# Gather, running sum and product: converting gathers into 64 slots instead of float32 gathers with casts on ScalarE

## The chip, the cores and the metric

The kernel runs on one core of one Trainium2 chip. The time is the device time of one execution in microseconds (us); of several executions the median is given. Beside it there is one execution taken by the hardware profiler, and all durations of single instructions come from that one.

The core has these engines, each with its own instruction stream: TensorE (PE in the profile, with its weight loads as PEld) multiplies matrices, VectorE (DVE) and ScalarE (ACT) work element by element, GpSimd (POOL) here issues the gathers, and SyncE (SP) issues the stores. 16 DMA engines move data between the main memory (HBM) and the on-chip memory (SBUF). Engines wait for each other through semaphores.

## The reference

```python
def reference(x, indices, w):        # x: 16 x 4096 x 512 float32, indices: 16 x 2048, w: 512 x 512
    B, S, D = x.shape
    b_idx = np.arange(B)[:, None]
    gathered = x[b_idx, indices, :].copy()
    cs = np.cumsum(gathered, axis=1)
    return np.matmul(cs, w).astype(np.float32)
```

For each of 16 batches 2048 rows are picked from 4096 by a sorted list of indices, summed up from the first row on, and each running sum is multiplied by `w`. 67.1 MB are read by the gathers and 67.1 MB are written.

## The kernel before, in words

The 16 x 2048 rows are 256 tiles (`T`) of 128 rows; a batch is 16 tiles (`NT`, also `U`, the length of a loop pass). Two tiles make a pair (`R = 2`, group `g`). In a pair the rows are not in tile order: the mask `ut` and the layout of `cst` deal them out so that each partition of the output holds two neighbouring rows, 4 KB in a row in HBM. In the first and the last pair (`PLAIN`, line 146) rows stay in order (mask `uq`), so that a tile can be finished without its partner.

A tile goes through these steps:

- `gather` (lines 127 to 143, GpSimd): one indirect DMA reads 128 rows of 2 KB into a float32 slot of `g32`. There are 16 slots (`NG`). From tile 16 on, the gather waits until the tile that last used its slot's pair has been cast (semaphore `s_c`, line 130).
- `cast` (lines 148 to 154, ScalarE): float32 to float16 into `g16` (8 pairs). The tables `casts` and `cast_by` (lines 114 to 125) say which casts come ahead of which drain; a cast runs up to 10 tiles (`FAR`) ahead of the drain.
- `sums` (lines 156 to 171, TensorE): four 128 x 128 products of the tile's columns with the mask give the running sums inside the tile, transposed, in PSUM buffer `pa` (four).
- `carry` (lines 173 to 198, VectorE): adds the last sum of the tile before and writes float16 into `cst`.
- `project` (lines 200 to 215, TensorE): four products with `w16`, 512 columns each, into PSUM buffer `pb` (four).
- `drain` (lines 217 to 220, ScalarE): copies `pb` to the output buffer `ob` (8 pairs).
- `store` (lines 222 to 236, SP): one DMA of 512 KB per pair, in the first and last pair one of 256 KB per tile. ScalarE waits for the store of eight pairs before (`s_o`, line 385) when it begins to refill a pair of `ob`.

The order on TensorE is written out ahead (lines 338 to 346): `lead` is how many tiles `sums` runs ahead of `project`, up to 4, less at both ends. On ScalarE the order is: wait for the slot of `ob` (at every second tile), the casts due, the drain. GpSimd's program is the 256 gathers in tile order. The middle of each program is a loop: 16 tiles a pass on TensorE, VectorE and ScalarE; the first and last tiles are written out.

Of the kernel before, what the change touches and what calls it, by code (L numbers as in the profile page):

```python
# [7 lines left out]
P = 128  # L8
FP32 = mybir.dt.float32
FP16 = mybir.dt.float16  # L10
# [23 lines left out]
def kernel(  # L34
# [7 lines left out]
    nc = tc.nc  # L42

    B, S, D = x.shape
    N = indices.shape[1]
    R = 2
# [15 lines left out]
    NO = 8  # L62
    U = NT
    assert U % NG == 0 and U % (R * NO) == 0 and U % NA == 0 and U % (R * NC) == 0 and U % NB == 0
    assert D == 512 and N % (R * P) == 0 and T % P == 0

    x_flat = x.rearrange("b s d -> (b s) d")
# [1 line left out]
    const = ctx.enter_context(tc.tile_pool(name="const", bufs=1))  # L69
# [31 lines left out]
    s_el = [sem(f"s_el{j}") for j in range(R)]  # L101
    s_ol = [sem(f"s_ol{j}") for j in range(R)]
    s_g = [sem(f"s_g{i}") for i in range(NG)]
# [10 lines left out]
    casts = []  # L114
    cast_by = []
    for u in range(T):
        far = min(FAR, 2 + u // 4, 2 + (T - 1 - u) // 4)
        casts.append([])
        while len(cast_by) <= min(u + far, T - 1):
            n = R if far > 4 and len(cast_by) % R == 0 else 1  # L120
            casts[u].append((len(cast_by), n))
            cast_by += [cast_by[-1] + 1 if cast_by else 1] * n

    for u in range(3 * U, T - 2 * U):
        assert casts[u] == [(t + U, n) for t, n in casts[u - U]]

    def gather(t):
        g, r = divmod(t, R)
        if t >= NG:
            pool.need(s_c, cast_by[R * (g + 1) - NG - 1])  # L130
        if t < FIRST:
            pool.need(s_first[g], 16)
            ap = idx_first[:, t, 0:1]
        else:
            pool.need(s_prep, t // P + 1)
            ap = idxg[:, t // P, t % P : t % P + 1]
        nc.gpsimd.indirect_dma_start(  # L137
            out=g32[g % (NG // R)][:, r, :],
            out_offset=None,
            in_=x_flat,  # L140
            in_offset=bass.IndirectOffsetOnAxis(ap=ap, axis=0),
            element_offset=(t // NT) * S * D,
        ).then_inc(s_g[t % NG], 16)


    PLAIN = (0, G - 1)

    def cast(t, n, first=None):
        g, r = divmod(t, R)
        for u in range(t, t + n):  # L150
            act.need(s_g[u % NG], 16 * (u // NG + 1), first)
        nc.scalar.copy(  # L152
            out=g16[g % NH][:, r : r + n], in_=g32[g % (NG // R)][:, r : r + n]
        ).then_inc(s_c, 1)

    def sums(t, u, first=None):
        g, r = divmod(t, R)
        tiles = None if first is None else R * first
        pe.need(s_c, cast_by[t] if first is None else cast_by[2 * U + t] - 2 * U // R, first)
        pe.need(s_d, t - NA + 1, tiles)  # L160
        for c in range(DC):
            if c == 1 and u is not None:
                pe.need(s_e, u - NB + 1, tiles)
            mm = nc.tensor.matmul(  # L164
                out=pa[t % NA][:, c],
                lhsT=g16[g % NH][:, r, c * P : (c + 1) * P],
                rhs=uq[:] if first is None and g in PLAIN else ut[:],
                start=(c == 0),
                stop=(c == DC - 1),
            )  # L170
        mm.then_inc(s_a, 1)
# [28 lines left out]
    def project(u, t, first=None):  # L200
        g, j = divmod(u, R)
        tiles = None if first is None else R * first
        pe.need(s_e, u - NB + 1, tiles)
        pe.need(s_d, u + 1 if first is None and g in PLAIN else R * (g + 1), tiles)
        for c in range(DC):
            if c == 2 and t is not None:
                pe.need(s_d, t - NA + 1, tiles)
            mm = nc.tensor.matmul(  # L208
                out=pb[u % NB][:],
                lhsT=cst[g % NC][:, c, j, :],  # L210
                rhs=w16[:, c, :],
                start=(c == 0),
                stop=(c == DC - 1),
            )
        mm.then_inc(s_b, 1)

    def drain(u, first=None):
        g, j = divmod(u, R)
        act.need(s_b, u + 1, first)
        nc.scalar.copy(out=ob[g % NO][:, j], in_=pb[u % NB][:]).then_inc(s_e, 1)  # L220

    def store(g):
        b, h = divmod(g, GB)
        rows = out[b, h * R * P : (h + 1) * R * P, :]
        if g in PLAIN:
            for j in range(R):
                sp.need(s_e, R * g + j + 1)
                done = s_ol[j] if g else (s_o[0], s_of)[j]
                nc.sync.dma_start(
                    out=rows[j * P : (j + 1) * P, :], in_=ob[g % NO][:, j]  # L230
                ).then_inc(done, 16)
# [24 lines left out]
    for g in range(G):  # L256
        store(g)
    for g in range(G - NO, G - 1):
        sp.need(s_o[g % NO], 16 * (g // NO + 1))
    for j in range(R):  # L260
        sp.need(s_ol[j], 16)


    nc.gpsimd.memset(ident[:], 1.0).then_inc(s_ut, 1)
# [3 lines left out]
        out=ident[:],  # L268
        in_=ident[:],
# [7 lines left out]
        out=ut[:],  # L277
# [72 lines left out]
    step = 2 * U  # L350
    for i in range(head + step, tail):
        assert order[i] == (order[i - step][0], order[i - step][1] + U)

    def run(i, first=None):
        is_sums, t = order[i]
        after = next((v for k, v in order[i + 1 :] if k != is_sums), None)
        if first is not None:
            t -= 2 * U
            after -= 2 * U
        if is_sums:  # L360
            sums(t, after, first)
        else:
            pe.need(s_wc, DC)
            project(t, after, first)

    for i in range(head):
        run(i)
    with nc.tensor.Fori(2 * U // R, (T - 2 * U) // R, U // R) as first:
        pe.new_pass()
        for i in range(head, head + step):  # L370
            run(i, first)
# [7 lines left out]
        act.need(s_w[c], 16)  # L379
        nc.scalar.copy(out=w16[:, c, :], in_=w32[:, c, :]).then_inc(s_wc, 1)  # L380
    def step(u, first=None):
        if u % R == 0:
            if first is None and u == R * NO:
                act.need(s_of, 16)
# [44 lines left out]
```

## Time and profile before

| | |
|---|---|
| Median of three runs | 454.9 us (454.53 to 455.43) |
| The profiled execution | 449.29 us, of which the span from first to last instruction is 447.5 us |
| Mean granted TensorE clock | 0.881 of full speed |
| TensorE, matmuls | busy 340.6 us, 76% of the span |
| ScalarE | busy 259.6 us: 256 drains of 0.598 us mean, 139 casts, 138.0 us in all |
| GpSimd | busy 243.9 us: 256 gathers, 0.946 us each |
| VectorE | busy 178.5 us |
| DMA | 135.69 MB, mean 303 GB/s |

How to read it: busy time is the time in which an engine executes; a wait is the time in which it stood before an instruction, with the one that released it. "remote", or "another core or an unknown queue", means that the profile has no record of the releaser; on one core it is a queue whose end was not recorded, or a wait that left no trace. A DMA share is the busy part of the 16 engines together. The page's rows of slices cut the span into 40 equal parts of 11.2 us, each digit in tenths. A busy engine need not be the bound: what counts is which wait ends last.

### The profile page before, as it was taken

The page shows a single profiled execution, that of the slowest core. Times are in us where ns is not written, and L with a number is a line of the kernel's source. Part 1 is how long each engine was busy: PE and PEld are TensorE (multiplying, and loading weights), DVE is VectorE, ACT ScalarE, POOL GpSimd, SP SyncE. Part 2 cuts the span into 40 slices and gives each one's busy share as a digit, 9 for nine tenths or more (in the row PEclk, how much of TensorE's full clock was granted, in tenths as well). Part 3 has the DMA queues.
Part 4 walks back from the last instruction along what each step waited for, and adds up shares of the span by engine and source line. Part 5 has one row for each costly group of instructions (what it writes and reads, how often), then busy time and mean ns, then how long its engine had stood idle before and what let it go on. Part 6 is the DMA issues. An engine that isn't in the chain of part 4 may idle for free.

```text
span 447.5 us, 6498 instructions
## 1 busy us (share of the span) xinstructions
PE 340.6 (76%) x2066; PEld 170.5 (38%) x2066; DVE 178.5 (40%) x263; ACT 259.6 (58%) x399; POOL 243.9 (54%) x266
## 2 busy tenths in 40 slices
PE   6354687578858887868788877987588888787995
PEld 2111244244424443424344434444244444344552
DVE  3103344224423454443345433444334444343652
ACT  3212467356636676655567655676456666555984
POOL 6771466575556555655656555655556655555300
PEclk9756789796999698988989889889889889799999
DMA  7874589897899888999989899988898988899974
GB/s 231 255 237 146 187 273 338 312 323 264 311 339 322 298 320 313 343 330 325 326 307 346 313 349 325 327 307 302 334 321 316 333 315 299 313 353 332 336 320 187
DMA packets 40619, 135.69 MB, mean 303 GB/s; under 512 B 6816, under 2 KB 7072, under 8 KB 40608
## 3 DMA queue, kind: packets, MB, share of 16 engines
q0 software_dynamic: 20480, 67.13, 47.3%
q1 hardware_dynamic: 19568, 67.91, 37.7%
q10 hardware_dynamic: 560, 0.53, 0.4%
q8 instruction: 5, 0.08, 0.1%
q14 instruction: 6, 0.05, 0.0%
HBM read 68.42 MB, written 67.11 MB: 303 GB/s over the span
## 4 chain that ended last, share of the span: by engine, by line
PE 70%; issue 12%; another core or an unknown queue 7%; ACT 6%; DVE 3%; DMA 1%; POOL 0%; ACTq 0%; DVEq 0%; SPq 0%
PE pb L208 54%; PE pa L164 16%; ACT g L152 3%; ACT ob L220 3%; DVE cst L196 3%; DMA g<-in_x_dram,idx_first 1%; DMA idx_first<-in_indices_dram 0%; DVE cst L183 0%; POOL g L137 0%; ACTq L26 0%; DVEq L26 0%; ACTq L393 0%; SPq L424 0%; SPq L90 0%
## 5 line engine op out<-in xcount | busy, mean ns | idle before, releaser
L137 POOL DMA_INDIRECT g<-in_x_dram,idxg x252 | 238.4, 946 | 173.1 <-ACT g L152 106.4
L208 PE MATMUL pb<-w,cst 128*128 128x512 f16 x1024 | 297.7, 417 | 44.0 <-issue 21.8
L196 DVE TENSOR_TENSOR cst<-pa,cst 128x512 f16<-128x512 f32 x240 | 166.0, 692 | 241.3 <-PE pa L164 152.4
L220 ACT COPY ob<-pb 128x512 f32<-128x512 f32 x256 | 144.9, 598 | 178.2 <-PE pb L208 118.8
L164 PE MATMUL pa<-ut,g 128*128 128x128 f16 x1008 | 113.1, 233 | 55.0 <-issue 21.3
L208 PEld LDWEIGHTS pb<-w,cst 128*128 128x128 f16 x1024 | 95.2, 106 | 126.2 <-issue 48.0
L152 ACT CAST g<-g 128x1024 f16<-128x1024 f32 (+1 forms) x139 | 138.0, 994 | 0.8 <-DMA g<-in_x_dram,idx_first 0.8
L164 PEld LDWEIGHTS pa<-ut,g 128*128 128x128 f16 x1008 | 81.5, 105 | 137.5 <-issue 45.5
L183 DVE CAST cst<-pa 128x512 f16<-128x512 f32 x16 | 11.0, 688 | 15.6 <-PE pa L164 14.0
L304 PE MATMUL pb<-zeros 128*128 128x512 f16 x16 | 5.7, 521 | 1.5 <-DVE zeros L308 1.5
L137 POOL DMA_INDIRECT g<-in_x_dram,idx_first x4 | 4.0, 994 | 1.6 <-issue 0.9
L304 PEld LDWEIGHTS pb<-zeros 128*128 128x128 f16 x16 | 1.9, 127 | 4.0 <-issue 1.9
L164 PE MATMUL pa<-uq,g 128*128 128x128 f16 x16 | 1.6, 220 | 1.7 <-ACT g L152 0.9
L377 ACT ACT_TABLE_LOAD x1 | 1.3, 1283 | 2.5 <-issue 2.5
L380 ACT CAST w<-w 128x512 f16<-128x512 f32 x2 | 1.1, 614 | 2.7 <-DMA w<-in_w_dram 2.7
L311 DVE CAST idxf<-idx 128x128 f32<-128x128 uint32 x2 | 0.5, 264 | 4.2 <-DMA idx<-in_indices_dram 4.2
L164 PEld LDWEIGHTS pa<-uq,g 128*128 128x128 f16 x16 | 1.0, 97 | 3.0 <-ACT g L152 1.5
L325 DVE CAST w<-w 128x512 f16<-128x512 f32 x2 | 0.8, 424 | 1.2 <-DMA w<-in_w_dram 1.2
L316 PE MATMUL pb<-ident,idxf 128*128 128x128 f32 x2 | 0.8, 376 | 0.5 <-DVE idxf L311 0.5
L316 PEld LDWEIGHTS pb<-ident,idxf 128*128 128x128 f32 x2 | 0.4, 186 | 1.4 <-DVE idxf L311 1.1
L308 DVE MEMSET zeros<- 128x256 uint32 x1 | 0.3, 272 | 1.1 <-SPq L90 1.1
L322 DVE CAST idxg<-pb 128x128 uint32<-128x128 f32 x2 | 0.6, 286 | 0.2 <-issue 0.2
(11 smaller groups left out, 2.1 us busy)
## 6 DMA issues: line engine op xcount, KB each, us to landing
out_dram<-ob SPq DMA_DIRECT2D x126, 512.0 KB
g<-in_x_dram,idxg POOLq DMA_INDIRECT x252
out_dram<-ob SPq DMA_DIRECT2D x4, 256.0 KB, 2.0
w<-in_w_dram ACTq DMA_DIRECT2D x2, 256.0 KB
w<-in_w_dram SPq DMA_DIRECT2D x2, 256.0 KB
idx<-in_indices_dram SPq DMA_DIRECT2D x2, 128.0 KB, 2.7
g<-in_x_dram,idx_first POOLq DMA_INDIRECT x4
idx_first<-in_indices_dram ACTq DMA_DIRECT2D x1, 2.0 KB, 2.1
```

The costliest lines, as they stand in the source:

```text
L137: nc.gpsimd.indirect_dma_start(out=g32[g % (NG // R)][:, r, :], out_offset=None, in_=x_flat, in_offset=bass.IndirectOffsetOnAxis(ap=ap, ax ...
L152: nc.scalar.copy(out=g16[g % NH][:, r : r + n], in_=g32[g % (NG // R)][:, r : r + n]).then_inc(s_c, 1)
L164: mm = nc.tensor.matmul(out=pa[t % NA][:, c], lhsT=g16[g % NH][:, r, c * P : (c + 1) * P], rhs=uq[:] if first is None and g in PLAIN else ...
L183: nc.vector.tensor_copy(out=dst, in_=src).then_inc(s_d, 1)
L196: nc.vector.tensor_tensor(out=dst, in0=src, in1=last, op=mybir.AluOpType.add).then_inc(s_d, 1)
L208: mm = nc.tensor.matmul(out=pb[u % NB][:], lhsT=cst[g % NC][:, c, j, :], rhs=w16[:, c, :], start=(c == 0), stop=(c == DC - 1),)
L220: nc.scalar.copy(out=ob[g % NO][:, j], in_=pb[u % NB][:]).then_inc(s_e, 1)
L304: nc.tensor.matmul(out=pb[NB - 1][:], lhsT=zeros[:, :P], rhs=zeros[:], start=True, stop=True)
L316: nc.tensor.transpose(out=pb[k % NB][:, :P], in_=idxf[:, k, :], identity=ident[:]).then_inc(s_pt, 1)
L325: nc.vector.tensor_copy(out=w16[:, c, :], in_=w32[:, c, :]).then_inc(s_wc, 1)
L377: nc.scalar.copy(out=spare[:], in_=zeros[:, :1])
L380: nc.scalar.copy(out=w16[:, c, :], in_=w32[:, c, :]).then_inc(s_wc, 1)
```

## The change

- The gather's destination becomes float16: the indirect DMA converts the rows while it moves them. `g32`, the casts on ScalarE, their tables and `s_c` go. `sums` waits for the gather's own semaphore `s_g`.
- `g16` becomes 32 pairs, 64 slots (`NG`). A gather waits until the gather 16 tiles before it (`FLY`) has landed, and at every eighth tile (`FREE`) until the `sums` that free the next eight slots are done (`s_a`). There are 32 gather semaphores (`NS`).
- The first two and the last two pairs are in row order (`PLAIN`).
- One store covers two pairs (`W = 2`), 1 MB, out of four double slots of `ob` (`NO`), so the output buffer keeps its size. The first two and the last two pairs are stored singly, the outermost ones per tile. ScalarE waits for a slot of `ob` at every fourth tile.
- `lead` is 1 within four tiles of both ends, then 2, and grows to 4 more slowly.
- TensorE's loop pass becomes 64 tiles (`V`). Waits inside it are counted from a base by `skip`.

The diff, cut to its core:

```diff
-    NG = 16
+    NG = 64
+    FLY = 16
+    NS = 32
+    FREE = 8
     LEAD = 4
-    FAR = 10
-    NH = 8
...
-    NO = 8
+    W = 2
+    NO = 4
     U = NT
+    V = NG
...
-    g32 = [const.tile([P, R, D], FP32, name=f"g32_{i}") for i in range(NG // R)]
-    g16 = [const.tile([P, R, D], FP16, name=f"g16_{i}") for i in range(NH)]
+    g16 = [const.tile([P, R, D], FP16, name=f"g16_{i}") for i in range(NG // R)]
     cst = [const.tile([P, DC, R, P], FP16, name=f"cst{i}") for i in range(NC)]
-    ob = [const.tile([P, R, D], FP32, name=f"ob{i}") for i in range(NO)]
+    ob = [const.tile([P, W, R, D], FP32, name=f"ob{i}") for i in range(NO)]
...
     def gather(t):
         g, r = divmod(t, R)
-        if t >= NG:
-            pool.need(s_c, cast_by[R * (g + 1) - NG - 1])
+        if t % FREE == 0:
+            pool.need(s_a, t + FREE - NG)
+        if t >= FLY:
+            pool.need(s_g[(t - FLY) % NS], 16 * ((t - FLY) // NS + 1))
...
         nc.gpsimd.indirect_dma_start(
-            out=g32[g % (NG // R)][:, r, :],
+            out=g16[g % (NG // R)][:, r, :],
...
-        ).then_inc(s_g[t % NG], 16)
-    PLAIN = (0, G - 1)
-    def cast(t, n, first=None):
...
+        ).then_inc(s_g[t % NS], 16)
+    PLAIN = (0, 1, G - 2, G - 1)
 
     def sums(t, u, first=None):
...
-        pe.need(s_c, cast_by[t] if first is None else cast_by[2 * U + t] - 2 * U // R, first)
+        skip = 0 if first is None else 2 * U
+        pe.need(s_g[t % NS], 16 * (t // NS + 1) - skip // R, first)
...
     def drain(u, first=None):
-        nc.scalar.copy(out=ob[g % NO][:, j], in_=pb[u % NB][:]).then_inc(s_e, 1)
-    def store(g):
+        nc.scalar.copy(out=ob[g // W % NO][:, g % W, j], in_=pb[u % NB][:]).then_inc(s_e, 1)
+    def store(g, n):
...
-        sp.need(s_e, R * (g + 1))
+        sp.need(s_e, R * (g + n))
+        done = {1: s_of, G - W: s_ol}.get(g, s_o[g // W % NO])
         nc.sync.dma_start(
-            out=rows.rearrange("(p j) d -> p j d", j=R), in_=ob[g % NO][:]
-        ).then_inc(s_o[g % NO], 16)
+            out=rows.rearrange(
+                "(g j p) d -> p g j d" if g in PLAIN else "(g p j) d -> p g j d", p=P, j=R
+            ),
+            in_=src[:, g % W : g % W + n],
+        ).then_inc(done, 16)
...
-        lead = min(LEAD, 1 + (u + 2) // 4, 1 + (T - 1 - u) // 6)
+        lead = 1 if min(u, T - 1 - u) < R * R else min(LEAD, 2 + (u + 4) // 16, 2 + (T - 1 - u) // 15)
...
-    with nc.tensor.Fori(2 * U // R, (T - 2 * U) // R, U // R) as first:
+    with nc.tensor.Fori(2 * U // R, (T - 2 * U) // R, V // R) as first:
...
     def step(u, first=None):
-        if u % R == 0:
-            act.need(s_o[u // R % NO], 16 * (u // R // NO), first)
-        for t, n in casts[u if first is None else 2 * U + u]:
-            cast(t if first is None else t - 2 * U, n, first)
+        if u % (W * R) == 0:
+            act.need(s_o[u // R // W % NO], 16 * (u // R // W // NO), first)
         drain(u, first)
```

More of the change, by code (lines that the diff above doesn't have):

```diff
@@ L61 @@
     NC = 4
-    NO = 8
+    W = 2
+    NO = 4
     U = NT
-    assert U % NG == 0 and U % (R * NO) == 0 and U % NA == 0 and U % (R * NC) == 0 and U % NB == 0
+    V = NG
+    assert V % NS == 0 and NS == 16 * R and 2 * U % NS == 0 and (T - 4 * U) % V == 0 and U % (W * R * NO) == 0 and U % NA == 0 and U % (R * NC) == 0 and U % NB == 0
     assert D == 512 and N % (R * P) == 0 and T % P == 0
@@ L100 @@
     s_idx = [sem(f"s_idx{k}") for k in range(KI)]
-    s_el = [sem(f"s_el{j}") for j in range(R)]
-    s_ol = [sem(f"s_ol{j}") for j in range(R)]
-    s_g = [sem(f"s_g{i}") for i in range(NG)]
+    s_ol = sem("s_ol")
+    s_g = [sem(f"s_g{i}") for i in range(NS)]
     s_o = [sem(f"s_o{i}") for i in range(NO)]
@@ L112 @@
     )
[L114 to L125, printed above, removed]
     def gather(t):
         g, r = divmod(t, R)
-        if t >= NG:
-            pool.need(s_c, cast_by[R * (g + 1) - NG - 1])
+        if t % FREE == 0:
+            pool.need(s_a, t + FREE - NG)
+        if t >= FLY:
+            pool.need(s_g[(t - FLY) % NS], 16 * ((t - FLY) // NS + 1))
         if t < FIRST:
@@ L142, in gather @@
             element_offset=(t // NT) * S * D,
-        ).then_inc(s_g[t % NG], 16)
-    PLAIN = (0, G - 1)
-    def cast(t, n, first=None):
[L149 to L154, printed above, removed]
+        ).then_inc(s_g[t % NS], 16)
+    PLAIN = (0, 1, G - 2, G - 1)
     def sums(t, u, first=None):
@@ L158, in sums @@
         tiles = None if first is None else R * first
-        pe.need(s_c, cast_by[t] if first is None else cast_by[2 * U + t] - 2 * U // R, first)
-        pe.need(s_d, t - NA + 1, tiles)
+        skip = 0 if first is None else 2 * U
+        pe.need(s_g[t % NS], 16 * (t // NS + 1) - skip // R, first)
+        pe.need(s_d, t - NA + 1 - skip, tiles)
         for c in range(DC):
             if c == 1 and u is not None:
-                pe.need(s_e, u - NB + 1, tiles)
+                pe.need(s_e, u - NB + 1 - skip, tiles)
             mm = nc.tensor.matmul(
                 out=pa[t % NA][:, c],
-                lhsT=g16[g % NH][:, r, c * P : (c + 1) * P],
-                rhs=uq[:] if first is None and g in PLAIN else ut[:],
+                lhsT=g16[g % (NG // R)][:, r, c * P : (c + 1) * P],
+                rhs=uq[:] if g in PLAIN else ut[:],
                 start=(c == 0),
@@ L202, in project @@
         tiles = None if first is None else R * first
-        pe.need(s_e, u - NB + 1, tiles)
-        pe.need(s_d, u + 1 if first is None and g in PLAIN else R * (g + 1), tiles)
+        skip = 0 if first is None else 2 * U
+        pe.need(s_e, u - NB + 1 - skip, tiles)
+        pe.need(s_d, (u + 1 if g in PLAIN else R * (g + 1)) - skip, tiles)
         for c in range(DC):
             if c == 2 and t is not None:
-                pe.need(s_d, t - NA + 1, tiles)
+                pe.need(s_d, t - NA + 1 - skip, tiles)
             mm = nc.tensor.matmul(
@@ L219, in drain @@
         act.need(s_b, u + 1, first)
[L220 to L222 removed]
+        nc.scalar.copy(out=ob[g // W % NO][:, g % W, j], in_=pb[u % NB][:]).then_inc(s_e, 1)
+    def store(g, n):
         b, h = divmod(g, GB)
[L224 to L225 removed]
+        rows = out[b, h * R * P : (h + n) * R * P, :]
+        src = ob[g // W % NO]
+        if g in (0, G - 1):
             for j in range(R):
                 sp.need(s_e, R * g + j + 1)
[L228 removed]
+                done = s_ol if g else (s_o[0], s_of)[j]
                 nc.sync.dma_start(
[L230 removed]
+                    out=rows[j * P : (j + 1) * P, :], in_=src[:, g % W, j]
                 ).then_inc(done, 16)
             return
[L233 removed]
+        sp.need(s_e, R * (g + n))
+        done = {1: s_of, G - W: s_ol}.get(g, s_o[g // W % NO])
         nc.sync.dma_start(
[L235 to L236 removed]
+            out=rows.rearrange(
[3 more added lines that the diff above has]
+        ).then_inc(done, 16)
     with nc.allow_non_contiguous_dma(reason="a few indices, one per partition"):
@@ L255 @@
         eng.dma_start(out=w32[:, c, :], in_=w[c * P : (c + 1) * P, :]).then_inc(s_w[c], 16)
[L256 to L261, printed above, removed]
+    for g in range(W):
+        store(g, 1)
+    for g in range(W, G - W, W):
+        store(g, W)
+    for g in range(G - W, G):
+        store(g, 1)
+    for i in range(G // W - NO, G // W - 1):
+        sp.need(s_o[i % NO], 16 * (i // NO + 1))
+    sp.need(s_ol, 16 * (R + W - 1))
     nc.gpsimd.memset(ident[:], 1.0).then_inc(s_ut, 1)
@@ L349 @@
     tail = order.index((False, T - 2 * U - 1)) + 1
-    step = 2 * U
+    step = 2 * V
     for i in range(head + step, tail):
-        assert order[i] == (order[i - step][0], order[i - step][1] + U)
+        assert order[i] == (order[i - step][0], order[i - step][1] + V)
     def run(i, first=None):
@@ L356, in run @@
         after = next((v for k, v in order[i + 1 :] if k != is_sums), None)
-        if first is not None:
-            t -= 2 * U
-            after -= 2 * U
         if is_sums:
@@ L381, in step @@
     def step(u, first=None):
-        if u % R == 0:
-            if first is None and u == R * NO:
-                act.need(s_of, 16)
-            act.need(s_o[u // R % NO], 16 * (u // R // NO), first)
-        for t, n in casts[u if first is None else 2 * U + u]:
-            cast(t if first is None else t - 2 * U, n, first)
+        if u % (W * R) == 0:
+            if first is None and u == W * R * NO:
+                act.need(s_of, 16 * (R + W - 2))
+            act.need(s_o[u // R // W % NO], 16 * (u // R // W // NO), first)
         drain(u, first)
```

## The prediction

> **What bounds the kernel now.** I read the slices of the page, the DMA queues, the chain of work, then a table by stage, the waits and the timeline. First the page:
>
> ```profile
> span 447.5 us, 6498 instructions
> ...
> DMA  7874589897899888999989899988898988899974
> ...
> q0 software_dynamic: 20480, 67.13, 47.3%
> q1 hardware_dynamic: 19568, 67.91, 37.7%
> ...
> PE 70%; issue 12%; another core or an unknown queue 7%; ACT 6%; DVE 3%; DMA 1%; POOL 0%; ACTq 0%; DVEq 0%; SPq 0%
> ```
>
> The chain names TensorE, but most of the span has DMA at 8 or 9 tenths. 67.1 MB are gathered and 67.1 MB stored; the two queues' packets fill 85% of 16 engines' span. In units of 4 KB a gather costs 0.473 x 16 x 447.5 us / 16384 = 207 ns, a store about 163 ns. Is DMA really full? The table by stage (columns: stretch, length, busy and count of PE, PEld, DVE, ACT, POOL, granted clock, DMA share, GB/s):
>
> ```profile
> 36.00:58.00 22.00, 13.15 (x62) 5.83 (x63) 6.79 (x11) 9.67 (x17) 8.10 (x9) 0.68 0.49 164
> 154.00:159.00 5.00, 4.96 (x38) 2.63 (x35) 0.78 (x2) 2.11 (x3) 2.93 (x4) 1.00 1.01 374
> 177.00:187.00 10.00, 8.21 (x58) 4.24 (x57) 3.08 (x5) 6.14 (x11) 6.42 (x7) 1.00 0.99 368
> 173.00:177.00 4.00, 3.77 (x17) 1.79 (x16) 3.24 (x5) 4.00 (x7) 1.89 (x2) 0.57 0.66 217
> ```
>
> Full, DMA moves some 368 GB/s; between the full stretches are holes (217), and from 58 to 420 us the mean is 320 GB/s. Neither is TensorE full: in warm bursts a tile (sums and project) takes 1.09 us, 279 us for 256 tiles. So the kernel is a DMA stream with holes. The waits show what makes them:
>
> ```profile
> POOL g L137 <- ACT g L152: 106.4, 38, 6.1
> ...
> ACT ob L220 <- remote: 49.3, 18, 7.5
> ```
>
> GpSimd waits 106 us for ScalarE's casts, since a float32 slot is free only once cast. Its gathers in the timeline come in runs, 1.25 us apart (0.946 busy, 0.30 between), then a pause of 3.5 to 4 us, about every 13.3 us in the middle of the run. ScalarE, in order, stands in a drain for what the profile can't name; the likely thing is the landing of an old store, whose slot it refills. A stalled drain thus stops the next gathers. At the start it is worst: GpSimd issued at 32.40 us and next at 39.49 us, while ScalarE's drains stood for 5.97, 6.64 and 7.52 us; at 58 us 33 gathers were issued and tile 16 was summed.
>
> **What the Trainium skill says.** "DMA: Bandwidth & Descriptors", section "SWDGE vs HWDGE vs iDMA": a cast in a DMA must be issued from GpSimd, as here; no price is given. Its section "Queues, rings and completion order": a DMA engine takes turns between queue rows by packets. The trace agrees in so far as gathers and stores advance together in the full stretches. "Collectives: The Full Stack", section "The bandwidth ceiling: the fold count and why AG ≠ RS ≠ AR": an add inside the DMA costs no cycles, its second read does; by analogy a cast would run at the pace of its reads. No cast is in this trace. "Runtime: NRT & Kernel Launch", section "Instruction fetch mechanics": TensorE holds 2048 instructions, the others 512, and a jump outside the window stalls. A loop body of 64 tiles at some 20 instructions is 1280, within it by that page.
>
> **The change part by part.**
>
> *Casts removed.* 139 ScalarE instructions, 138.0 us, go; ScalarE keeps 256 drains x 0.59 = 151 us. Its busy share is no bound (58%), so by itself this is worth nothing; its worth is that a gather no longer waits for ScalarE.
>
> *Gathers.* 256 as before, each reads the same 256 KB and writes half. Issue: 1.25 us x 256 = 320 us if the descriptors of a cast cost no more. Before, satisfied slot waits fitted in the 0.30 us between two gathers; the new one, for the landing of 16 tiles back, replaces one of that kind. Behind it on GpSimd stand only gathers, whose slots lie up to 64 tiles ahead, so it starves TensorE only once that lead is used up. Data side unknown: halved writes could bring the packet to the store's 163 ns (-21%, -45 us); a cast unit could double it (+212 us). I take no change: the reads, which stay, set the pace by the analogy above.
>
> *Start.* GpSimd runs on through the drains' stalls: from 3.2 us at 1.25 us, 44 gathers by 58 us, 11 more than now, 2.9 MB or 8 us of full DMA. I leave tile 16 at 58 us, since the drains' stalls have no cause that the change removes. Moved by then: 44 + 15 tiles x 0.262 = 15.4 MB of 134.2.
>
> *Middle.* The lead of the gathers over the sums is 44 - 16 = 28 tiles. With 16 gathers waiting in DMA at all times, a stall of ScalarE leaves no hole. Gathers end when 28 tiles (7.3 MB) are unstored: (134.2 - 15.4 - 7.3) MB / 368 GB/s = 303 us, so at 361 us. TensorE needs 240 x 1.09 = 262 us for its part, 290 at a clock of 0.90: hidden, but if it stayed at half clock (2.1 us a tile, as at 57 to 60 us) it would be the bound.
>
> *End.* The last 28 tiles lack only TensorE and stores: 28 x 1.09 = 31 us, above the stores' 28 x 0.262 MB / 414 GB/s = 18 us (rate of 422 to 428 us). Then 4 us from the last drain to the end, as now: 361 + 31 + 4 = **396 us** of span.
>
> *Row order of four pairs, shorter lead, larger stores.* Sums that may wait for one tile instead of a pair let the first and last projects start up to a tile (1.1 us) earlier. The second pair's stores have 2 KB runs, two DMAs among 68. Two pairs per store leaves the bytes, halves SP's issues (0.33 us each, SP waits 262 us anyway), and makes ScalarE wait for 1 MB slots, four instead of eight: same 16 tiles, freed in steps twice as coarse. The deep gather queue covers that; without the cover it is a hole of up to two tiles (2.8 us) per slot round. Together I book 0, from -3 to +10 us. The 64-tile loop cuts TensorE's loop turns from 12 to 3, with no stall of a jump visible now: 0.
>
> Span 396 against 447.5 is -51.5. The profiled execution took 449.3 us (1.8 beyond its span), the median of the runs shown is 454.9, 5.6 above that. I carry both over: 396 + 1.8 + 5.6 = **404 us**.
>
> **The rivals.**
>
> *The cast slows the transfer* (ends slower). Place: the gather packets, 212 us of all 16 engines' time. It decides at +24% (51.5 / 212): 257 instead of 207 ns per 4 KB. At +40% the median is 404 + 85 = 489; doubled, 616. For it: DMA is the one resource with nothing to spare, and a cast must touch each element. Against: nothing in the profile; the analogy. GpSimd's descriptors have a like point, 1.69 us per gather instead of 1.25 ((447.5 - 15) / 256).
>
> *The cast makes the packets cheaper.* Half the bytes land in SBUF. If gathers come down to 163 ns, 45 us go from the middle until GpSimd's 320 us of issue and the end's 31 us bound it: some 365 to 385 us. Against: stores and gathers differ now in the direction of HBM as much as in size.
>
> *The change doesn't do what it says*: holes stay because they come from store landings and coarser 1 MB slots, not from gather slots. Then DMA stays at 320 GB/s in the middle and only the start's 8 us come: 447 us, from 430 to 460. For it: "ACT ob <- remote" in the middle (35.8 us of the 49.3 lie after 58 us). Against: in the holes GpSimd is the one that stands still, and TensorE has work.
>
> **How the numbers follow.** The forecast: 0.54. Its own range is 380 to 430: a lead of 10 to 60 tiles instead of 28 gives spans of 380 to 408 by the same sum (medians 387 to 416), a packet 6% off moves 13 us. Cheaper packets 0.10; dearer transfer or descriptors 0.28, of which 0.25 slower, 0.01 the same, 0.02 faster; no effect 0.08 (0.03, 0.03, 0.02: faster, same, slower). Faster 0.69, same 0.04 (within 0.2%, what a measurement here can tell), slower 0.27. The range must cut into the dear cast: below 378 lie about 0.07, above 475 about 0.13.
>
> **What would show it.** Right: gathers 1.25 us apart without pauses up to the mid 50s of us; no DMA slice below 9 from about 60 to 360 us and some 360 GB/s; the gather queue's share x span still near 212 us; GpSimd waiting for gather landings, not for ScalarE; gathers ending 25 to 60 tiles before the last project, TensorE dense after. Wrong: a gather queue well over 212 us of engine time at the same rows, or DMA full at under 320 GB/s (dear cast); DMA_INDIRECT well above 946 ns on GpSimd; DMA holes again with ScalarE's drains before them (store slots); TensorE at half clock for long.

## The result and the profile after

The changed kernel takes 473.7 us (median of four runs, 471.31 to 474.2), the kernel before 455.2 us in the same comparison (454.53 to 456.12): 1.0395 times as long, with a 95% interval of 1.0355 to 1.0435. The profiled execution took 473.79 us, its span is 472.1 us. The prediction had said 404 us.

One thing has to be known ahead of every number below: the chips differ. On the chip of this comparison, and on chip 15 of the experiments, the kernel before takes 452 to 455 us; on chips 8 and 12 it takes 353 us. The two kinds are called late chips and prompt chips here, for a reason that the traces show. Each experiment is compared with the kernel before on the same chip at the same time.

The page of the changed kernel, the lines that answer to those shown of the kernel before, and GpSimd's row of slices:

```profile
span 472.1 us, 6042 instructions
...
POOL 7777777323665656566566665655656655000000
...
DMA  7988888446999999999999999999999999566556
...
q0 software_dynamic: 36864, 33.57, 51.2%
...
PE 64%; another core or an unknown queue 24%; DVE 5%; issue 5%; ACT 1%; DVEq 0%; SPq 0%
```

A slice is 11.8 us. GpSimd first runs at 7 tenths, the most it reaches here, for seven slices, then drops to 3 and 2; it has nothing left to do in the last six. DMA has a hole at 83 to 106 us and works at half in the last six slices. In the chain an unknown releaser now holds 24% of the span; it was 7%. The table by stage (columns as in the prediction):

```profile
36.00:58.00 22.00, 1.89 (x6) 0.79 (x7) 0.69 (x1) 0.58 (x1) 16.67 (x18) 0.50 0.88 129
...
200.00:250.00 50.00, 39.45 (x255) 20.24 (x254) 21.74 (x32) 17.64 (x33) 29.49 (x32) 0.93 1.02 255
...
420.00:440.00 20.00, 20.00 (x147) 11.24 (x146) 12.25 (x18) 10.69 (x20) 0.00 (x0) 1.00 0.62 247
```

From 36 to 58 us, where the kernel before did 62 matmuls and 17 ScalarE instructions, there are 6 matmuls, one carry and one drain, beside 18 gathers. In the middle a tile takes 50 us / 32 = 1.56 us. At the end TensorE is dense, with no gathers left. The waits (total us, times, longest):

```profile
DVE cst L179 <- remote: 142.1, 25, 21.7
...
PEld pb L192 <- DVE cst L179: 118.2, 31, 32.6
...
ACT ob L204 <- remote: 85.3, 21, 21.1
...
POOL g L127 <- PE pa L147: 64.6, 18, 14.0
```

VectorE stands 142 us before carries, and the profile cannot name the releaser. Besides the carry before it, a carry waits only for `sums`, through `s_a`. So "remote" is no queue here: the increment comes so long after its matmul that the profile does not put the two together. The timeline of the stalled stretch (start, duration, engine, line, operation, and in brackets the idle time before it) shows where those `sums` were:

```profile
21.05 1.89 PE L192 MATMUL pb<-w,cst 128*128 128x512 f16 x4 [5.04 <-DVE cst L179]
22.73 1.06 PE L147 MATMUL pa<-ut,g 128*128 128x128 f16 x8
56.11 1.89 PE L192 MATMUL pb<-w,cst 128*128 128x512 f16 x4 [32.32 <-DVE cst L179]
57.79 0.63 PE L147 MATMUL pa<-ut,g 128*128 128x128 f16 x4
58.22 1.91 PE L192 MATMUL pb<-w,cst 128*128 128x512 f16 x4
...
55.36 0.69 DVE L179 TENSOR_TENSOR cst<-pa,cst 128x512 f16<-128x512 f32 x1 [21.01 <-remote]
66.56 0.69 DVE L179 TENSOR_TENSOR cst<-pa,cst 128x512 f16<-128x512 f32 x1 [10.51 <-remote]
88.96 0.69 DVE L179 TENSOR_TENSOR cst<-pa,cst 128x512 f16<-128x512 f32 x1 [21.71 <-remote]
...
44.16 0.58 ACT L204 COPY ob<-pb 128x512 f32<-128x512 f32 x1 [19.01 <-remote]
77.76 0.58 ACT L204 COPY ob<-pb 128x512 f32<-128x512 f32 x1 [33.02 <-issue]
99.46 0.59 ACT L204 COPY ob<-pb 128x512 f32<-128x512 f32 x1 [21.11 <-remote]
...
81.79 0.94 POOL L127 DMA_INDIRECT g<-in_x_dram,idxg  x1 [0.31 <-issue]
89.20 0.94 POOL L127 DMA_INDIRECT g<-in_x_dram,idxg  x1 [6.47 <-remote]
...
112.88 0.94 POOL L127 DMA_INDIRECT g<-in_x_dram,idxg  x1 [14.04 <-PE pa L147]
```

Follow TensorE's work in its order: project of tile 3 (21.05 us), sums of tiles 5 and 6 (22.73), project 4 (56.11), sums 7 (57.79), project 5 (58.22). Their successors start at 44.16 (drain 3), 55.36 and 66.56 (carries 5 and 6), 77.76 (drain 4), 88.96 (carry 7) and 99.46 us (drain 5): the same order, one by one, 11.2 us apart (10.5 the last time), over two engines that share nothing but TensorE as their source. For five of the six the trace has the record of the increment, and each of them starts 0.02 us after it (carry 5 at 55.36 us, the increment at 55.34); for drain 4 there is no record. So it is the increment itself that comes late: 32 us after the matmuls of sums 5. The other direction is prompt: carry 5 ends at 56.05 us, and project 4 starts at 56.11. Meanwhile GpSimd issued 64 gathers without a stop, one per 1.243 us, up to 82.7 us, when its slots were full.

So the data lay ready and TensorE had started what it could; its completions were late, and came one at a time. The ends of matmuls are modelled in the profile, so it does not show whether a matmul's own end or only its signal is late.

With this in view the kernel before shows the same at its start, on a smaller scale:

```profile
29.13 0.61 PE L164 MATMUL pa<-ut,g 128*128 128x128 f16 x4 [5.43 <-ACT g L152]
...
35.68 0.69 DVE L196 TENSOR_TENSOR cst<-pa,cst 128x512 f16<-128x512 f32 x1 [11.91 <-remote]
...
37.12 0.58 ACT L220 COPY ob<-pb 128x512 f32<-128x512 f32 x1 [7.52 <-remote]
```

The sums at 29.13 us are those of tile 6, the carry at 35.68 us is carry 6.

### The profile page after: what moved, and what is told of

Read it like the earlier page. It is cut to its first block, busy times and chain, and to the rows that moved or that the text cites. A ratio compares the mean times of both kernels' runs of the same rounds, so it can differ in the third digit from the quotient of the medians.

```text
span 472.1 us, 6042 instructions
## 1 busy us (share of the span) xinstructions
PE 322.3 (68%) x2066; PEld 167.4 (35%) x2066; DVE 178.3 (38%) x263; ACT 146.0 (31%) x260; POOL 241.9 (51%) x266
## 3 DMA queue, kind: packets, MB, share of 16 engines
q0 software_dynamic: 36864, 33.57, 51.2%
## 4 chain that ended last, share of the span: by engine, by line
PE 64%; another core or an unknown queue 24%; DVE 5%; issue 5%; ACT 1%; DVEq 0%; SPq 0%
PE pb L192 47%; PE pa L147 16%; DVE cst L179 5%; PE pb L296 1%; ACT ob L204 1%; PE pb L308 0%; DVEq L26 0%; DVE zeros L300 0%; DVEq L411 0%; SPq L92 0%
## 5 line engine op out<-in xcount | busy, mean ns | idle before, releaser
L192 PE MATMUL pb<-w,cst 128*128 128x512 f16 x1024 | 285.6, 404 | 117.5 <-DVE cst L179 109.0
L204 ACT COPY ob<-pb 128x512 f32<-128x512 f32 x256 | 143.4, 590 | 316.1 <-PE pb L192 179.8
L192 PEld LDWEIGHTS pb<-w,cst 128*128 128x128 f16 x1024 | 92.1, 102 | 195.6 <-DVE cst L179 118.2
L147 PE MATMUL pa<-ut,g 128*128 128x128 f16 x992 | 105.4, 228 | 25.2 <-issue 14.9
L147 PEld LDWEIGHTS pa<-ut,g 128*128 128x128 f16 x992 | 79.6, 103 | 95.9 <-issue 33.5
L147 PEld LDWEIGHTS pa<-uq,g 128*128 128x128 f16 x32 | 2.4, 98 | 1.6
L147 PE MATMUL pa<-uq,g 128*128 128x128 f16 x32 | 2.9, 219 | 0.0
```

Source lines behind the costliest of these rows:

```text
L147: mm = nc.tensor.matmul(out=pa[t % NA][:, c], lhsT=g16[g % (NG // R)][:, r, c * P : (c + 1) * P], rhs=uq[:] if g in PLAIN else ut[:], star ...
L192: mm = nc.tensor.matmul(out=pb[u % NB][:], lhsT=cst[g % NC][:, c, j, :], rhs=w16[:, c, :], start=(c == 0), stop=(c == DC - 1),)
L204: nc.scalar.copy(out=ob[g // W % NO][:, g % W, j], in_=pb[u % NB][:]).then_inc(s_e, 1)
```

## Experiments

Two theories stood at the start. The first: **the unbroken issue of gathers** delays TensorE's completions, and the 64 slots allow an unbroken run of 64 to 72 gathers where 16 float32 slots had stopped GpSimd after 24, at 33 us. The second: **the conversion** does it, by the DMA work (the gather queue has 36864 packets now, 144 for a gather of 128 rows instead of 80) or by the bytes and packets waiting in the DMA engines.

### First set, chip 12 (kernel before: 352.7 us)

*lead16*: a gather waits until the sums are within 16 tiles of it, in steps of two; all else is the changed kernel.

```diff
-        if t % FREE == 0:
-            pool.need(s_a, t + FREE - NG)
+        if t % R == 0:
+            pool.need(s_a, t + R - 16)
```

> The changed kernel, but a gather waits until the sums are within 16 tiles of it (checked at every second tile); slots, gathers in flight and everything else as they are. Theory 1 (TensorE's completions reach VectorE and ScalarE late while GpSimd issues gathers back to back without a wait, and the late signals pile up): GpSimd is stopped after 16 gathers, the pile clears, tile 16 is summed by about 60 us instead of 113 us, and the time is 410 to 435 us. Theory 2 (the converting transfer itself is the whole loss): the start hardly changes and the time stays at 460 to 475 us.

*plain64*: 64 float32 slots and no conversion. TensorE reads the upper half of each float32 as a bfloat16, so the numbers are coarser than the reference's; no engine does extra work.

```diff
-    g16 = [const.tile([P, R, D], FP16, name=f"g16_{i}") for i in range(NG // R)]
+    g16 = [const.tile([P, R, D], FP32, name=f"g16_{i}") for i in range(NG // R)]
...
-                lhsT=g16[g % (NG // R)][:, r, c * P : (c + 1) * P],
+                lhsT=g16[g % (NG // R)][:, r, :].bitcast(BF16)[:, 2 * c * P + 1 : 2 * (c + 1) * P : 2],
```

> The changed kernel with plain float32 gathers into 64 float32 slots, no conversion anywhere: the sums read the upper halves of the float32 numbers as bfloat16, so the numbers are coarser. Theory 1: the start is as bad as with the conversion, tile 16 summed after 90 us or later, and only the middle gains from the cheaper packets (about 1.42 instead of 1.5 us a tile), so 445 to 465 us. Theory 2: without the conversion the start is like that of the kernel before or better, and the time is 390 to 420 us.

*narrow*: each gather moves 128 pieces of 128 columns instead of 128 rows of 512, with the conversion; the slots are zeroed once at the start, and the gathers wait for that. Three quarters of the gathered data are left out, and most of what is summed is zero.

```diff
         nc.gpsimd.indirect_dma_start(
-            out=g16[g % (NG // R)][:, r, :],
+            out=g16[g % (NG // R)][:, r, :128],
             out_offset=None,
-            in_=x_flat,
+            in_=x.rearrange("b s (k d) -> (b s k) d", d=128),
```

> The changed kernel, each gather moving 128 of the 512 columns (512 B read, 256 B written a row), the slots filled with zeros by VectorE first, which delays the start by some 10 us; so most of what is multiplied is zero. Same number of gathers, rows and packets, a quarter of the bytes. If the late signals come from the issue of gathers on GpSimd: the start stays as long, tile 16 summed after 90 us or later, and the time is 400 to 440 us. If they come from the bytes in the DMA queues: tile 16 is summed by 50 us and the time is 335 to 370 us.

*fly3start*: for the first 64 gathers at most three are in flight instead of 16.

```diff
-        if t >= FLY:
-            pool.need(s_g[(t - FLY) % NS], 16 * ((t - FLY) // NS + 1))
+        fly = 3 if t < NG else FLY
+        if t >= fly:
+            pool.need(s_g[(t - fly) % NS], 16 * ((t - fly) // NS + 1))
```

> The changed kernel, but the first 64 gathers have at most 3 in flight instead of 16: GpSimd pauses for a landing before each of them, while the lead over the sums may grow to 64 as before. Theory 1: the pauses are enough for the signals to get through, tile 16 is summed by about 60 us, and the time is 410 to 440 us. Rival (the deep lead or the work in DMA, not the unbroken issue, delays TensorE's signals): tile 16 later than 90 us, 460 us or more.

| run | us | ratio to the kernel before | 95% |
|---|---|---|---|
| lead16 | 354.97 | 1.0066 | 1.0046 to 1.0086 |
| plain64 | 348.26 | 0.9866 | 0.983 to 0.990 |
| narrow | 351.42 | 0.9967 | 0.9953 to 0.998 |
| fly3start | 383.87 | 1.0875 | 1.077 to 1.098 |

The expectations were made for a chip on which the kernel before takes 455 us, and the runs told nothing of the stall, for this chip has none: tile 16 is summed by 32.2 us in lead16 and by 30.5 us in plain64. lead16, plain64 and fly3start missed. narrow, at 351.42 us with tile 16 at 42.7 us, lies in the range that I had set for the bytes in the queues as the cause; without a stall in any run it is no sign for them. What the runs do tell is the prompt chip's bound. The last gather of plain64 is issued at 322.3 us: 256 x 1.245 us = 319 us of issue from 3 us on. GpSimd's issue is the bound here, with a start of 3 us and some 24 us after the last gather. With a quarter of the bytes (narrow) the issue keeps its pace, 317.5 us from the first gather to the last; it begins 15.6 us later, after the zeroing, and only 13.4 us follow the last gather. fly3start misses on its own account: with three in flight the first 64 gathers take some 33 us more than in after2 below.

### Second set, chip 8 (353.3 us): the two kernels as they are, and both edits together

> The changed kernel as it is, a second time, since the kernel before took 352.7 us in the last experiments and 455.2 us in the comparison of the two kernels. If the late signals belong to the chip on which the two were compared and this one has none: tile 16 is summed by 40 us, the end of a sums and the start of its carry are 0.3 us apart all along, 350 to 362 us, and before at 352 to 354 us. If this chip has them: 471 to 475 us, and before at 454 to 456 us. Theory 2 (the converting transfer is the loss): slower than before by 3 to 5% on either.

> The kernel before as it is, for a profile on the same chip as the changed one. Without late signals: 352 to 354 us, no pauses of GpSimd of 3.5 us in every 13, DMA at 9 tenths or more. With them: 454 to 456 us and the pauses.

*plainlead* joins the edits of plain64 and lead16 (coarser numbers again).

> Plain float32 gathers into 64 float32 slots whose upper halves the sums read as bfloat16 (coarser numbers), and a gather waits until the sums are within 16 tiles of it. On a chip without late signals: 345 to 352 us, 1 to 2% faster than before, with the conversion's dearer packets gone. On a chip with them: 380 to 420 us, since the lead keeps GpSimd from running on unbroken. Theory 2: 345 to 352 us on either.

after2 took 354.81 us, a ratio of 1.0039 (1.0023 to 1.0055); before2 352.35 us in a single execution; plainlead 348.43 us, 0.9843 (0.979 to 0.990). All three came as expected, plainlead as both theories had it. On a prompt chip the change costs 0.4%. Three views of after2 beside those of the changed kernel on the late chip: the page, VectorE's timeline and the table by stage. The last line is before2.

```profile
span 353.9 us, 6042 instructions
...
q0 software_dynamic: 36864, 33.57, 58.6%
...
DMA 55%; POOL 28%; issue 10%; PE 5%; ACT 0%; POOLq 0%; SPq 0%
```

```profile
25.15 0.69 DVE L179 TENSOR_TENSOR cst<-pa,cst 128x512 f16<-128x512 f32 x1 [0.39 <-PE pa L147]
```

```profile
200.00:250.00 50.00, 43.62 (x305) 22.13 (x304) 26.38 (x39) 22.72 (x39) 37.61 (x40) 1.00 1.13 299
...
150.00:200.00 50.00, 45.15 (x313) 23.14 (x312) 26.73 (x40) 39.84 (x60) 37.87 (x40) 1.00 1.03 413
```

The same program has no unknown releaser in the chain, and VectorE stands 0.4 us before a carry where it stood 11 to 22 us on the late chip, although GpSimd runs as unbroken as there (40 gathers in 50 us). From the start of the last matmul of a sums to its carry it is 0.26 us throughout, from that of a project to its drain 0.42 us, 0.50 at most (where the engine had been idle). The kernel before has no holes either on this chip: 40 gathers in 50 us, the last one issued at 323.0 us, and 413 GB/s, so GpSimd's issue bounds it as well. The table holds a warning too: DMA reaches a share of 1.13 with the conversion. The 1.02 in the middle of the changed kernel on the late chip looked like a full DMA, and is not.

This pair also prices the converting gathers. Share x span of the gather queue: 58.6% x 353.9 = 207.4 us here, in before2 49.8% x 350.6 = 174.6 us; +19%. On the late chip 51.2% x 472.1 = 241.7 us against 47.3% x 447.5 = 211.7; +14%. plain64 (chip 12), which differs from after2 in the gathers and in how the sums read them, has 50.0% x 346.5 = 173.3 us, so +20% for after2, and 0.9866 against 1.0039 puts them at some 1.7% of the time on a prompt chip. A plain gather has 64 packets of 4 KB beside 16 of 4 bytes, a converting one 128 of 1 KB beside 16; whether the conversion or the greater number of packets costs this, no run tells apart.

### Third set, chip 15 (453.7 us, a late chip): the lead limited, and the stores as before

*lead24* is lead16 with 24 in place of 16.

> The changed kernel, but a gather waits until the sums are within 24 tiles of it, checked at every second tile. On a chip where TensorE's completions come late (before at 455 us): GpSimd has to stop at the start, so tile 16 is summed by 75 us instead of 113 us, and the time is 415 to 445 us. On a chip without (before at 353 us): the lead never reaches 24 in the middle, 353 to 356 us, like the changed kernel. Theory 2 (the conversion is the loss): 460 us or more on the first kind.

*onepair* takes the larger stores back: one pair per store, eight slots.

```diff
-    W = 2
-    NO = 4
+    W = 1
+    NO = 8
...
-        done = {1: s_of, G - W: s_ol}.get(g, s_o[g // W % NO])
+        done = {W - 1: s_of, G - W: s_ol}.get(g, s_o[g // W % NO])
```

> The changed kernel with one pair per store and eight slots of one pair, as before; all else as changed. If the larger stores have a part in the loss, this is 3 us or more faster than the changed kernel (354.8 us where before takes 353 us, 473.7 us where before takes 455 us); if they are worth nothing, as the prediction booked, it is within 3 us of it. On a chip with late completions the start stays long, tile 16 summed after 100 us.

lead24 took 418.02 us, a ratio of 0.9237 (0.9065 to 0.9409), as the first theory expected. Its table by stage and its VectorE timeline:

```profile
36.00:58.00 22.00, 13.34 (x84) 7.19 (x85) 8.20 (x12) 5.86 (x10) 11.37 (x13) 0.73 0.75 158
...
200.00:250.00 50.00, 41.23 (x266) 20.71 (x264) 23.52 (x34) 17.79 (x33) 31.25 (x34) 0.93 1.06 269
```

```profile
42.84 1.49 DVE L179 TENSOR_TENSOR cst<-pa,cst 128x512 f16<-128x512 f32 x2 [13.37 <-remote]
45.94 0.69 DVE L179 TENSOR_TENSOR cst<-pa,cst 128x512 f16<-128x512 f32 x1 [1.61 <-PE pa L147]
...
49.16 0.69 DVE L179 TENSOR_TENSOR cst<-pa,cst 128x512 f16<-128x512 f32 x1 [0.40 <-PE pa L147]
```

The first stall, of 13.4 us, is still there, for 28 gathers, up to 38 us, are still unbroken. Then GpSimd stands at its limit, the completions arrive, and carries follow at 0.40 us. There are 84 matmuls where the changed kernel had 6. Tile 16 is summed by 57.3 us instead of 113.8, 56.5 us earlier; the span is 472.1 - 417.0 = 55.1 us shorter. The whole gain is the start. Nothing but a wait was added, and the conversion, the slots and the stores stayed. Behind the start the lags stay: from 120 to 380 us the carries for which VectorE stood idle come 3.5 us in the median after the last matmul of their sums, up to 6.1 us, and a tile takes 50 us / 34 = 1.47 us. A limited lead cures the stall, not the chip's lag.

onepair took 481.24 us, 1.0634 (1.040 to 1.087), where the changed kernel had 473.7 in the first comparison; I had expected it within 3 us of that or faster. The two were measured at different times, so the 7.5 us are not a price of the smaller stores; but the loss does not come from the larger ones. The start is the same (tile 16 at 113.6 us). The changed kernel itself was not run on chip 15; onepair, which differs from it in the stores alone, takes its place beside lead24: tile 16 at 113.6 against 57.3 us at the same time on the same chip.

### Fourth set, chip 15 (451.9 us): the conversion and the DMA load on a late chip

*plain64late*, *narrowlate* and *plainlead2* are the kernels plain64, narrow and plainlead once more.

> Plain float32 gathers into 64 float32 slots, no conversion (the sums read the upper halves as bfloat16), for a chip with late completions (before at 450 to 456 us). If the unbroken issue of gathers alone delays TensorE's completions: the start is as long as with the conversion, tile 16 summed after 95 us, 445 to 465 us in all. If the conversion's packets (144 a gather instead of 80) have a part: a shorter interval between completions in the start than 11 us, tile 16 summed between 60 and 95 us, 410 to 445 us. On a chip without late completions: 347 to 350 us again.

> Gathers of 128 of 512 columns, with the conversion, slots zeroed first (most of what is multiplied is zero). On a chip with late completions: if the issue and its packets delay the completions, tile 16 is summed after 100 us and the time is 430 us or more; if the bytes in the DMA queues do, tile 16 is summed by 60 us and the time is below 390 us. On a chip without: 350 to 352 us again.

> Plain float32 gathers into 64 slots, sums reading bfloat16, a lead of at most 16 tiles over the sums. On a chip with late completions: GpSimd stops after 16 gathers, tile 16 is summed by 55 us, 385 to 415 us, faster than the converting kernel with a lead of 24 (418.0 us). On a chip without: 347 to 349 us again.

plain64late took 476.42 us and narrowlate 484.23, each in a single execution; plainlead2 took 409.42, a ratio of 0.906 (0.9021 to 0.9099). Tile 16 is summed by 113.2 us in plain64late and by 126.2 us in narrowlate, whose gathers begin 15.6 us later: the start is as long as with the conversion and all bytes. First plain64late, without conversion: VectorE's timeline and the middle.

```profile
45.59 0.69 DVE L180 TENSOR_TENSOR cst<-pa,cst 128x512 f16<-128x512 f32 x1 [18.95 <-remote]
56.79 0.69 DVE L180 TENSOR_TENSOR cst<-pa,cst 128x512 f16<-128x512 f32 x1 [10.51 <-issue]
79.19 0.69 DVE L180 TENSOR_TENSOR cst<-pa,cst 128x512 f16<-128x512 f32 x1 [21.71 <-issue]
```

```profile
250.00:300.00 50.00, 39.78 (x257) 20.28 (x255) 20.93 (x31) 16.93 (x31) 30.14 (x32) 0.94 0.93 333
```

Then narrowlate, with a conversion of a quarter of the data:

```profile
53.52 0.69 DVE L181 TENSOR_TENSOR cst<-pa,cst 128x512 f16<-128x512 f32 x1 [14.76 <-remote]
75.92 0.69 DVE L181 TENSOR_TENSOR cst<-pa,cst 128x512 f16<-128x512 f32 x1 [21.71 <-remote]
```

```profile
58.00:70.00 12.00, 0.71 (x5) 0.36 (x3) 0.00 (x0) 0.58 (x1) 9.04 (x10) 0.64 0.29 27
...
250.00:300.00 50.00, 39.42 (x265) 20.68 (x264) 21.52 (x32) 17.82 (x33) 29.76 (x32) 0.96 0.66 185
```

The step is 11.2 us (56.79 - 45.59) or twice that, a drain coming between, with 80 packets per gather or 144, and in narrowlate with DMA busy at 0.29 and moving 27 GB/s. So neither conversion nor packets nor bytes nor a full DMA makes completions late. What the three have in common is GpSimd, issuing a gather every 1.24 us, and the deep lead. The second theory falls for the stall.

Is it the issue or the lead? fly3start would part them, but it ran on a prompt chip only. The trace of the changed kernel on the late chip helps, since its middle has the lead without the unbroken issue: at 200 us the gathers are 57 tiles ahead of the sums, no fewer than at 82 us (55), while GpSimd stops after every eighth gather. There the lags grow within a run of eight to some 6.5 us and are gone soon after each stop (carry 76 starts 6.51 us after the last matmul of its sums, carry 81 0.35 us). So a deep lead alone does not make the stall.

The late traces also tell a count. In each of them the signals held up at the start have all come by 1.41 to 1.42 us per gather issued until then, reckoned from the first gather:

| run | gathers | first gather, us | all signals in, us | us per gather |
|---|---|---|---|---|
| plainlead2 | 20 | 3.18 | 31.64 | 1.42 |
| kernel before | 24 | 3.20 | 37.17 | 1.42 |
| lead24 | 28 | 3.23 | 42.84 | 1.41 |
| changed kernel | 72 | 3.17 | 104.43 | 1.41 |
| onepair | 72 | 3.18 | 104.53 | 1.41 |
| plain64late | 72 | 3.18 | 104.48 | 1.41 |
| narrowlate | 72 | 18.80 | 120.10 | 1.41 |

This holds wherever GpSimd stood in between, with the conversion and without. My estimate from this table: on a late chip something takes about 1.40 us for each gather (61.6 us more for 44 gathers more, changed kernel against lead24), GpSimd issues one per 1.243 us, and TensorE's signals pass in full only when it has caught up. The step of 11.2 us is then eight gathers at 1.40 us.

The middle agrees: 32 or 33 gathers in 50 us in the changed kernel, in plain64late and in narrowlate alike, at DMA shares of 1.02, 0.93 and 0.66. I had expected 445 to 465 us of plain64late, since fewer packets would speed up the middle; DMA does not set the pace there. GpSimd runs for eight gathers (`FREE`), stops, mostly for 2.3 to 3.4 us, until TensorE's signals are in, and goes on, about 12.5 us for eight tiles, while the slots ahead of TensorE are full.

plainlead2 beats both kernels: tile 16 is summed by 46 us, and 0.906 compares with 0.9237 of lead24. With 0.9843 on chip 8 it is faster than the kernel before on both kinds of chip, at coarser numbers. With full numbers, lead24 is the better one on the late chip (lead16 was not run there), and lead16 gives 0.7% away on the prompt one.

## Why the prediction was wrong

The predicted span was 396 us: gathers to 361, then 35. In the trace the last gather is issued at 396.3 us, and 75.8 us follow: 35 and 41 us more, 76 in all.

- **The failed step is "Start"**: "I leave tile 16 at 58 us, since the drains' stalls have no cause that the change removes." They had a cause that the change enlarges. The stalls of ScalarE between 14 and 37 us in the kernel before, and of VectorE (11.9 us before its carry at 35.68), were late completions during 24 unbroken gathers, and the slot waits that I booked as the cost to be removed were what let the signals catch up. With 72 gathers up to 98.8 us tile 16 came at 113.8 us instead of 58. My reading of the lines was loose as well: of the three stalls that I set beside GpSimd's pause, only the third (up to 37.12 us) falls into it; the other two fall into its unbroken run. The first half of the step was right: GpSimd did run at 1.24 us per gather through the stalls.
- **What bounds the kernel**: I read "ACT ob <- remote" as the landing of an old store. A drain waits for `s_b` of TensorE as well, and that was it. At the start the program alone rules stores out: the three stalled drains are of tiles 2 to 4, and no slot of `ob` is refilled before tile 16. From 58 to 420 us each of the 49 waits of over 1 us before a drain ends at an increment of `s_b` in the trace. There carries come some 3 us (median of those for which VectorE stood idle, 100 to 390 us) and up to 8.5 us after the last matmul of their sums. The holes in DMA were thus no sign of a DMA stream with a hiccup; on the late chip TensorE's signals hold up the whole loop. On a prompt chip the kernel before has no holes, and the 320 us of issue that I named and took for hidden bound both kernels.
- **Gathers**: "Behind it on GpSimd stand only gathers" is right of GpSimd's queue, and misleading: what stood behind the gathers were TensorE's signals.
- **Middle**: 14 us of GpSimd's pause up to 112.9 us, and 283.4 us from there to the last gather instead of 184 x 1.43 = 263 us (my 303 us for 212 gathers), 20 us more, make up 34 of the 35 us.
- **End**: the lead had run to its limit while TensorE stood. After the last gather 65 drains follow instead of my 28: 37 x 1.09 = 40 us, the 41 above. The rate of 1.09 us per tile holds. One sum of mine does not come out: a lead of 10 tiles gives 389 us of span by the same steps, not 380.
- **Rivals.** None is the case. The slower one, the dear cast, has a real price, +14 to 20%, under the +24% at which it was to decide. Here the Trainium skill's page "Collectives: The Full Stack" (section "The bandwidth ceiling: the fold count and why AG ≠ RS ≠ AR"), by which a transfer with an add is slower for its second read and not for the add's cycles, did not carry over to a converting gather. One sign that I had set for this rival came, DMA at 1.02 with 255 GB/s, and narrowlate shows that it was no bound. "Holes stay" came nearest, but named stores. The shares given, 0.27 for slower, rested on the wrong mechanism.
- **Right**: GpSimd's price of a gather (0.94 us, as before), no stall seen from the 64-tile loop, and a gain behind the start: from tile 16 to the end 472.1 - 113.8 = 358.3 us against 447.5 - 57.8 = 389.7 in the kernel before. The change brings 31 us there and loses 56 at the start; 25 is the difference of the spans. lead24, with 38 gathers issued by tile 16 instead of 73, has 359.7 us behind it, so the gain is not a gift of the stall. That the casts' removal is worth nothing by itself was not tried: no run removes them alone.

## What to carry to other kernels

A slot limit that looks like a cost may be what paces an engine; before deepening a buffer, ask what else moves while its producer is stopped. A limit of the producer's lead, by a wait on the consumer, cost 0.3% at most where it was not needed (lead16 at 1.0066 against 1.0039, with intervals that overlap) and took 11% off where it was (lead24 at 0.9237 against 1.0395 of the changed kernel, each against the kernel before at its own time). When an engine waits for an unknown releaser, list every semaphore that the waiting instruction needs and look whether the work behind one of them had long been done: here the successors of one engine started in its order at a fixed distance, and that told late signals from late work. And run a kernel on more than one chip before its holes are put down to the program.

## What the runs showed of the hardware that was not expected

- While GpSimd issues gathers back to back, one per 1.243 us, TensorE's completions reach VectorE, ScalarE and GpSimd late on some chips, in order and up to 11.2 us apart. On chips 8 and 12 the lag from the start of the last matmul stays at 0.26 us (carry) and 0.42 us (drain) under the same issue; on a late chip it is the same 0.26 and 0.42 once the gathers are over. The kernel before takes 453 us on the one kind, 353 us on the other.
- What in the chip does it stays open. GpSimd's stop from 82.7 to 89.2 us did not shorten the step (77.76 to 88.96 us), which fits the estimate above: something that needs 1.40 us per gather was still behind at 88.96 us. The test of it was not made: gathers issued with idle time between them, at 1.40 us or more each, with the full lead, on a late chip. Nor was it tried to give the completions another way. The traces differ in one thing more: of the 4096 increments with which the gathers report their landing, those of the seven late executions hold 766 to 1674, those of the prompt ones all. Whether the recording has a part in the lag is open too. That the chip of the first comparison is of chip 15's kind is taken from its times (455 and 453 us) and its 11.2 us steps; lead24 was not run on it.
- A gather that converts float32 to float16 has 144 packets for 128 rows instead of 80, and its queue's time grows by 19% (prompt chip) or 14% (late chip), while half the bytes land. GpSimd's own time for it doesn't change.
- The kernel before moves 413 GB/s on a prompt chip (100 to 200 us), above the 368 GB/s that I had taken for full.
